# Accumulating transfers of a column pair's blocks, each tied to the low weight part of a later row pair

## The chip, the cores and the metric

The kernel runs on one core of a Trainium2 chip, written in Bass with the Tile layer. The metric is the device time of one execution in microseconds; the median of the runs counts. The kernel works in float32, which it splits into a high and a low part for TensorE.

## The reference

A two-layer decoder trunk on 256 tokens of width 2048: layer 0 is RetNet retention, layer 1 multi-head latent attention (MLA), each followed by a squared-ReLU MLP of width 8192, each added to the residual stream.

```python
for layer in range(DEPTH):                       # DEPTH = 2
    h = rms_norm(x, norm_mix[layer])
    if layer < N_A_LAYERS:
        x = x + retention(h, ret_w_in[layer], ret_w_out[layer], ret_cos, ret_sin)
    else:
        ...                                      # shared keys and values, once
        x = x + mla_attention(h, ...)
    x = x + sq_relu_mlp(rms_norm(x, norm_mlp[layer]), mlp_w1[layer], mlp_w2[layer])

def sq_relu_mlp(h, w1, w2):
    return jnp.square(jax.nn.relu(h @ w1)) @ w2
```

## The kernel before

All weights are streamed once from HBM, 479 MB in total, and every weight is split on the way: `split` makes a high part on ScalarE (line 184) and the low part, weight minus high part, on VectorE (line 185). TensorE then runs three matmuls for each product: high by high, high by low, low by high (lines 360 to 362).

Most products go through `gemm_pair`. It works on a *column pair*: 1024 output columns, two column blocks of 512, times two token blocks of 128, so four output blocks c11, c12, c21, c22. It goes through the inner dimension in *row pairs* of 256 rows, one call of `quad` each: one load of 1 MB (line 289, on the SyncE queue, three buffers `raw`), the split in parts, and the matmuls. A plain row pair has eight products, so 24 matmuls; a "seven" uses Strassen's scheme in the Winograd form, with seven products, 21 matmuls, and three sums of weight blocks on VectorE ahead of them (lines 319 to 324). Which row pairs are sevens stands in lists: `ODD` means the second, fourth, sixth and eighth, `SEVEN` the fourth, sixth and eighth, and so on.

At the end of a column pair `pair_out` copies the accumulators out of PSUM (line 377) and makes the sums of Winograd's form (lines 379 to 384). The result is two tiles for each of four blocks, eight tiles of 128 by 512, whose sums are the blocks. They lie in the pool `f2k`, 14 tiles that are used in turn.

The residual stream lives in HBM, in eight tiles `x_home` of 128 by 512. A product whose result isn't the last addition of its layer part is added there by `to_home`: eight transfers of 256 KB with an addition on the way (line 146), issued on GpSimd's queue, one for each tile. The result tiles of a column pair are sent by `send` in the order c11, c21, c12, c22, then the second tile of each. This is done for the first half of the retention's output product (name `ro0`, 2 column pairs) and for three of the four groups of each MLP's second product (names `d0_0` to `d1_2`, 2 column pairs each): 14 times eight transfers. For the last half or group the blocks of the residual stream are read back (`x_tiles`, line 138, also on GpSimd's queue) and added on VectorE (line 469).

What is issued when is set by a small clock. `later(n, fn)` puts a function into a list that is due n ticks on, and each row pair ends with one `tick`, which runs what is due. So the program hands out the eight transfers one per row pair, over the eight row pairs of the column pair that follows (`ro01`'s run under the next head's value and gate product, those of a group's second column pair under the next group's first up-projection `u`). The tick orders the program; what each engine's queue looks like in the end is also up to the Tile layer's scheduler. On the chip an instruction starts when it is first in its engine's queue and the semaphores it waits for have come.

GpSimd's queue holds little else: the norms' `rstd` (lines 162 and 164), the tables at the start, the reads and writes of `x_home`.

Of the kernel before, what the change touches and what calls it, by code (L numbers as in the profile page):

```python
# [16 lines left out]
ALU = mybir.AluOpType  # L17
# [49 lines left out]
def yoco(ctx: ExitStack, tc: tile.TileContext, a):  # L67
    nc = tc.nc
# [22 lines left out]
        return pool.tile([P, 2, 2, S], dtype, tag="act", bufs=24, name=name)  # L91


    queue = []
    clock, count = [0], itertools.count()

    def later(n, fn):
        queue.append((clock[0] + n, next(count), fn))
# [6 lines left out]
    def tick():  # L105
        clock[0] += 1
        while queue and min(q[0] for q in queue) <= clock[0]:
            run_first()
# [19 lines left out]
    x_home = [[dram.tile([P, 512], F32, name=f"xh_{t}_{b}") for b in range(NB)] for t in range(NT)]  # L128
# [14 lines left out]
    def to_home(c, p):  # L143

        def send(t, j, i):
            nc.gpsimd.dma_start(x_home[t][2 * p + j], c[t][j][i], accum_op=ALU.add)  # L146

        for n, (i, j, t) in enumerate(itertools.product(range(2), range(2), range(NT))):
            later(n, lambda i=i, j=j, t=t: send(t, j, i))
# [31 lines left out]
    def split(h, l, src, scale=None):  # L181

        if scale is None:
            nc.scalar.copy(h, src)  # L184
            return nc.vector.tensor_tensor(l, src, h.bitcast(F32), op=ALU.subtract)  # L185
        nc.scalar.activation(h, src, AF.Copy, scale=scale)
        return nc.vector.scalar_tensor_tensor(
            l, src, scale, h.bitcast(F32), op0=ALU.mult, op1=ALU.subtract
        )
# [16 lines left out]
    def stream(w, chunk, cols, name, use, done=None, before=None):  # L206

        raw = pool.tile([P, 2048], F32, tag="raw", bufs=3, name=f"{name}_raw")
        if before is None:
            nc.sync.dma_start(raw[:, :cols], w[chunk])  # L210
        n = cols // 2
        for half in range(2):
            wh = pool.tile([P, 1024], F32R, tag="wh", bufs=5, name=f"{name}_wh{half}")
            wl = pool.tile([P, 1024], F32R, tag="wl", bufs=5, name=f"{name}_wl{half}")
            cuts = 1
            if before is not None:
                cuts = 1 if half else 2
                m = n // cuts
                for i in range(cuts):
                    lo = half * n + i * m  # L220
                    nc.sync.dma_start(raw[:, lo : lo + m], w[chunk][:, lo : lo + m])
                    if i == 0:
                        before(half)
            m = n // cuts
            for i in range(cuts):
                lo = half * n + i * m
                split(wh[:, i * m : (i + 1) * m], wl[:, i * m : (i + 1) * m], raw[:, lo : lo + m])
            use(half, wh, wl)
        if done is not None:
            queue.append((clock[0] + 1, -1, done))  # L230
        tick()

    def piece(w, chunk, acc, act, g, nk, nb, name, before=None, done=None):

        if before is None:
            need(act, 2 * g + 2)

        def use(half, wh, wl):
            for j in range(2):
                k = g * 4 + half * 2 + j  # L240
                rh, rl = (v[:, j * nb : (j + 1) * nb] for v in (wh, wl))
                for t in range(NT):
                    ah, al = (act[k // 2][:, j, i, t * P : (t + 1) * P] for i in range(2))
                    nc.tensor.matmul(acc[t], ah, rh, start=k == 0, stop=False)
                    nc.tensor.matmul(acc[t], ah, rl, start=False, stop=False)
                    nc.tensor.matmul(acc[t], al, rh, start=False, stop=k == nk - 1)

        stream(
            w, chunk, 4 * nb, f"{name}{g}", use, done and (lambda: done(acc)),
            before and (lambda half: before(2 * g + half)),  # L250
        )

    def gemm_t(w, chunk0, act, nk, name, done):

        acc = accs(512, name)
        n = nk // 8
        for g in range(n):
            need(act, 4 * g + 4)

            def use(half, wh, wl):  # L260
                for j in range(4):
                    k = g * 8 + half * 4 + j
                    a = act[k // 2][:, k % 2]
                    for f in range(2):
                        cols = slice(j * 256 + f * P, j * 256 + (f + 1) * P)

                        def low():
                            nc.tensor.matmul(acc[f][:, 0:S], wl[:, cols], a[:, 0], start=False, stop=False)

                        if k > 0:  # L270
                            low()
                        nc.tensor.matmul(  # L272
                            acc[f], wh[:, cols], a.rearrange("p i s -> p (i s)"), start=k == 0, stop=k == nk - 1
                        )
                        if k == 0:
                            low()

            stream(w, chunk0 + g, 2048, f"{name}{g}", use, (lambda: done(acc)) if g == n - 1 else None)

    def queued_behind(ins, before):  # L280
        tc.add_manual_dep(
            ins.ins, before.ins.name,
            mybir.DependencyInfo(mybir.DependencyClass.NoSync, mybir.DependencyReason.DATA), reason="order",
        )

    def quad(w, chunk, x, mm, name):

        raw = pool.tile([P, 2048], F32, tag="raw", bufs=3, name=f"{name}_raw")
        nc.sync.dma_start(raw, w[chunk])
        v, more = x  # L290

        def a(t, k):
            return [v[:, k, i, t * P : (t + 1) * P] for i in range(2)]

        def s(n):
            return [more[:, n // 2, i, n % 2 * P : (n % 2 + 1) * P] for i in range(2)]

        def parts(src, n, part, after=None):
            wh = pool.tile([P, 1024], F32R, tag="wh", bufs=5, name=f"{name}_wh{part}")
            wl = pool.tile([P, 1024], F32R, tag="wl", bufs=5, name=f"{name}_wl{part}")  # L300
            low = split(wh[:, : n * 512], wl[:, : n * 512], src)
            if after is not None:
                queued_behind(low, after)
            return [[i[:, j * 512 : (j + 1) * 512] for i in (wh, wl)] for j in range(n)]

        if more is None:
            b11, b22 = parts(raw[:, 0:1024], 2, 0)
            mm("c11", a(0, 0), b11)
            mm("c21", a(1, 0), b11)
            mm("c12", a(0, 1), b22)  # L310
            mm("c22", a(1, 1), b22)
            b12, b21 = parts(raw[:, 1024:], 2, 1)
            mm("c12", a(0, 0), b12)
            mm("c22", a(1, 0), b12)
            mm("c11", a(0, 1), b21)
            mm("c21", a(1, 1), b21)
            return
        u = [pool.tile([P, 2, 512], F32, tag="us", bufs=2, name=f"{name}_u{i}") for i in range(2)]
        nc.vector.tensor_tensor(
            u[0], raw[:, 0:1024].rearrange("p (i n) -> p i n", i=2),  # L320
            raw[:, 1024:1536].unsqueeze(1).to_broadcast([P, 2, 512]), op=ALU.add,
        )
        nc.vector.tensor_tensor(u[1][:, 0], u[0][:, 0], raw[:, 512:1024], op=ALU.add)
        summed_up = nc.vector.tensor_tensor(u[1][:, 1], u[1][:, 0], raw[:, 1536:], op=ALU.add)  # L324
        b11, b22 = parts(raw[:, 0:1024], 2, 0, summed_up)
        mm("p1", a(0, 0), b11)
        mm("c12", s(3), b22)
        (b21,) = parts(raw[:, 1536:], 1, 1, summed_up)
        mm("c11", a(0, 1), b21)
        u2, u4 = parts(u[1].rearrange("p i n -> p (i n)"), 2, 2)  # L330
        mm("c21", a(1, 1), u4)
        mm("p6", s(2), u2)
        u1, u3 = parts(u[0].rearrange("p i n -> p (i n)"), 2, 3)
        mm("p5", s(1), u1)
        mm("p7", s(0), u3)
# [856 lines left out]
```

## Time and profile before

| | |
|---|---|
| runs (us) | 2511.81, 2500.82, 2499.96; median 2500.82 |
| profiled execution | 2506.1 us, span 2504.3 us |
| mean granted TensorE clock | 0.994 of full speed |
| busy share of TensorE, VectorE, ScalarE, GpSimd | 98%, 88%, 66%, 10% |
| read from HBM, written | 479.14 MB, 39.85 MB |
| accumulating transfers (line 146) | 112 of 256 KB |

How to read the rows: PE is TensorE, DVE VectorE, ACT ScalarE, POOL GpSimd, SP SyncE; a "q" behind the name is its queue of transfers. Times are in microseconds from the span's start. A timeline row gives start, length, engine, line, operation, output and inputs; in square brackets it has how long the engine stood idle before it and what ended that. A row of waits gives who waited for whom, then the total, the number of times and the longest. Buffer numbers and column pair numbers are left out of names, so `d_c` stands for every column pair of the second product, `u_c` for the first. A matmul's length is longer than its step, since matmuls overlap; the distance of two starts is what counts.

### The profile page before, as it was taken

To read this page: it belongs to the slowest core of one execution; us is meant where nothing else is said; L and a number is where in the kernel's file an instruction comes from. 1 tells how busy PE (TensorE), PEld (TensorE's weight loads), DVE (VectorE), ACT (ScalarE), POOL (GpSimd) and SP (SyncE) were. 2 spreads that over 40 slices of the span, in tenths; PEclk is the share of its full clock that TensorE was granted. 3 is DMA by queue.
4 is the path that set the end of the run, shared out by engine and by line. 5 is a ranking of instruction groups with operands and counts; after the bars stand their busy time and mean duration, and the time that the engine had idled before them with its cause. 6 is when DMAs were issued, how large, how long until landed. Compare 5 with 4: busy or idle time off the path is not lost.

```text
span 2504.3 us, 31661 instructions
## 1 busy us (share of the span) xinstructions
PE 2463.4 (98%) x11614; PEld 2069.5 (83%) x11614; DVE 2199.7 (88%) x2892; ACT 1648.3 (66%) x2297; POOL 251.6 (10%) x308
## 2 busy tenths in 40 slices
PE   9999999999999999999999999999999999999999
PEld 7788888888888878888788888998888788788787
DVE  6799999889889989989889998776999889899896
ACT  6566666556667757677667777666677567576673
POOL 7300011000010110110110101110000101101100
PEclk9999999999999999999999999999999999999999
DMA  8555577555565775775875555444556857857764
GB/s 310 191 200 189 189 220 243 193 188 208 202 233 183 217 251 183 235 231 194 239 249 200 195 194 180 161 147 160 190 200 206 243 203 213 251 184 226 241 214 167
DMA packets 93403, 521.04 MB, mean 208 GB/s; under 512 B 11072, under 2 KB 12224, under 8 KB 40000
## 3 DMA queue, kind: packets, MB, share of 16 engines
q1 hardware_dynamic: 71856, 472.83, 53.6%
q0 software_dynamic: 21248, 46.15, 9.5%
q8 instruction: 91, 1.49, 0.2%
q14 instruction: 64, 0.52, 0.1%
q10 hardware_dynamic: 144, 0.05, 0.0%
HBM read 479.14 MB, written 39.85 MB: 207 GB/s over the span
## 4 chain that ended last, share of the span: by engine, by line
PE 79%; DVE 10%; DMA 6%; ACT 2%; issue 2%; POOL 1%; DVEq 0%; ACTq 0%; POOLq 0%
PE u_c L361 6%; PE u_c L362 6%; PE u_c L360 6%; PE d_c L361 5%; PE d_c L362 5%; PE d_c L360 5%; DMA u_raw<-in_mlp_w 4%; PE rp_c L360 2%; PE rp_c L362 2%; PE rp_c L361 2%; PE rq_acc L272 2%; PE rk_acc L272 2%; DMA d_raw<-in_mlp_w 2%; DVE d_wl L185 2%; PE ro_c L361 1%
## 5 line engine op out<-in xcount | busy, mean ns | idle before, releaser
L185 DVE TENSOR_TENSOR d_wl<-d_raw,d_wh 128x1024 fp32r<-128x1024 f32 (+1 forms) x256 | 278.7, 1114 | 27.6 <-ACT d_wh L184 27.5
L184 ACT CAST d_wh<-d_raw 128x1024 fp32r<-128x1024 f32 (+1 forms) x256 | 241.6, 975 | 86.8 <-PE d_c L362 45.1
L185 DVE TENSOR_TENSOR u_wl<-u_raw,u_wh 128x1024 fp32r<-128x1024 f32 (+1 forms) x256 | 277.3, 1110 | 16.0 <-ACT u_wh L184 16.0
L361 PE MATMUL u_c<-u_wl,n 128*128 128x512 f32 x712 | 279.2, 392 | 11.1 <-DVE u_wl L185 11.1
L184 ACT CAST u_wh<-u_raw 128x1024 fp32r<-128x1024 f32 (+1 forms) x256 | 240.8, 971 | 74.5 <-PE u_c L362 48.9
L360 PE MATMUL u_c<-u_wh,n 128*128 128x512 f32 x712 | 279.8, 394 | 0.0
L362 PE MATMUL u_c<-u_wh,n 128*128 128x512 f32 x712 | 278.7, 391 | 0.0
L361 PE MATMUL d_c<-d_wl,hid 128*128 128x512 f32 x660 | 258.8, 392 | 6.5 <-DVE d_wl L185 6.5
L360 PE MATMUL d_c<-d_wh,hid 128*128 128x512 f32 x660 | 259.6, 393 | 0.0
L362 PE MATMUL d_c<-d_wh,hid 128*128 128x512 f32 x660 | 258.1, 391 | 0.0
L184 ACT CAST u_wh<-u_u 128x1024 fp32r<-128x1024 f32 x104 | 107.7, 1054 | 114.5 <-DVE u_u L324 60.4
L184 ACT CAST d_wh<-d_u 128x1024 fp32r<-128x1024 f32 x100 | 103.6, 1055 | 101.2 <-DVE d_u L324 54.1
L361 PEld LDWEIGHTS u_c<-u_wl,n 128*128 128x128 f32 x712 | 134.6, 189 | 42.0 <-DVE u_wl L185 14.7
L362 PEld LDWEIGHTS u_c<-u_wh,n 128*128 128x128 f32 x712 | 134.3, 189 | 27.9
L360 PEld LDWEIGHTS u_c<-u_wh,n 128*128 128x128 f32 x712 | 134.5, 189 | 27.5
L361 PEld LDWEIGHTS d_c<-d_wl,hid 128*128 128x128 f32 x660 | 124.7, 189 | 33.5 <-DVE d_wl L185 8.4
L184 ACT CAST rp_wh<-rp_raw 128x1024 fp32r<-128x1024 f32 x112 | 104.1, 946 | 68.8 <-PE rp_c L362 42.4
L362 PEld LDWEIGHTS d_c<-d_wh,hid 128*128 128x128 f32 x660 | 124.7, 189 | 26.0
L360 PEld LDWEIGHTS d_c<-d_wh,hid 128*128 128x128 f32 x660 | 124.7, 189 | 25.6
L185 DVE TENSOR_TENSOR u_wl<-u_u,u_wh 128x1024 fp32r<-128x1024 f32 x104 | 123.8, 1218 | 9.6 <-ACT u_wh L184 9.6
L146 POOL DMA_DIRECT2D xh<-d_c x48 | 41.9, 948 | 844.1 <-ACT d_c L377 843.7
L185 DVE TENSOR_TENSOR d_wl<-d_u,d_wh 128x1024 fp32r<-128x1024 f32 x100 | 119.0, 1218 | 5.0 <-ACT d_wh L184 5.0
(567 smaller groups left out, 6694.9 us busy)
## 6 DMA issues: line engine op xcount, KB each, us to landing
u_raw<-in_mlp_w SPq DMA_DIRECT2D x128, 1024.0 KB, 5.2
d_raw<-in_mlp_w SPq DMA_DIRECT2D x120, 1024.0 KB, 4.9
rp_raw<-in_ret_w_gv SPq DMA_DIRECT2D x56, 1024.0 KB, 4.9
ro_raw<-in_ret_w_out SPq DMA_DIRECT2D x32, 1024.0 KB, 5.0
uq_raw<-in_mla_w_uq SPq DMA_DIRECT2D x24, 768.0 KB, 4.2
rq_raw<-in_ret_w_qk SPq DMA_DIRECT2D x16, 1024.0 KB, 5.3
rk_raw<-in_ret_w_qk SPq DMA_DIRECT2D x16, 1024.0 KB, 4.8
xh<-d_c POOLq DMA_DIRECT2D x48, 256.0 KB, 5.5
```

Of the source, the lines that this page charges most:

```text
L146: nc.gpsimd.dma_start(x_home[t][2 * p + j], c[t][j][i], accum_op=ALU.add)
L184: nc.scalar.copy(h, src)
L185: return nc.vector.tensor_tensor(l, src, h.bitcast(F32), op=ALU.subtract)
L272: nc.tensor.matmul(acc[f], wh[:, cols], a.rearrange("p i s -> p (i s)"), start=k == 0, stop=k == nk - 1)
L360: nc.tensor.matmul(dst, ah, bh, start=n == 0, stop=False)
L361: nc.tensor.matmul(dst, ah, bl, start=False, stop=False)
L362: nc.tensor.matmul(dst, al, bh, start=False, stop=n == total[key] - 1)
```

## The change

`low_part` remembers the latest low part that `split` made of a weight in `quad` (and in `stream`, which the other products use). Each accumulating transfer gets a semaphore wait on that instruction. As `send` runs in the tick at the end of a row pair, each of the eight transfers waits for the last low part of its own row pair.

```diff
-    queue = []
+    queue, low_part = [], [None]
...
         def send(t, j, i):
-            nc.gpsimd.dma_start(x_home[t][2 * p + j], c[t][j][i], accum_op=ALU.add)
+            ins = nc.gpsimd.dma_start(x_home[t][2 * p + j], c[t][j][i], accum_op=ALU.add)
+            tc.add_manual_dep(
+                ins.ins, low_part[0].ins.name,
+                mybir.DependencyInfo(mybir.DependencyClass.Sync, mybir.DependencyReason.SCHED_ONLY), reason="spaced",
+            )
 
         for n, (i, j, t) in enumerate(itertools.product(range(2), range(2), range(NT))):
             later(n, lambda i=i, j=j, t=t: send(t, j, i))
...
-                split(wh[:, i * m : (i + 1) * m], wl[:, i * m : (i + 1) * m], raw[:, lo : lo + m])
+                low_part[0] = split(wh[:, i * m : (i + 1) * m], wl[:, i * m : (i + 1) * m], raw[:, lo : lo + m])
...
-            low = split(wh[:, : n * 512], wl[:, : n * 512], src)
+            low = low_part[0] = split(wh[:, : n * 512], wl[:, : n * 512], src)
```

The order in which instructions stand on TensorE, VectorE, ScalarE and SyncE is the same before and after. On GpSimd the transfers of a column pair stand in the order c11, c21, c12, c22; before, the scheduler had them as c22, c12, c11, c21.

## The prediction

> **What bounds the kernel now.** I read the page's first part, then who waited for whom on TensorE and VectorE, then the chain that ended last, then timelines and windows around the transfers.
>
> ```profile
> span 2504.3 us, 31661 instructions
> PE 2463.4 (98%) x11614; PEld 2069.5 (83%) x11614; DVE 2199.7 (88%) x2892; ACT 1648.3 (66%) x2297; POOL 251.6 (10%) x308
> PE u_c L361 <- DVE u_wl L185: 11.1, 8, 2.2
> PE d_c L361 <- DVE d_wl L185: 6.5, 4, 2.5
> DVE u_u L319 <- DMA u_raw<-in_mlp_w: 30.0, 18, 3.7
> DVE d_u L319 <- DMA d_raw<-in_mlp_w: 22.4, 15, 4.5
> ```
>
> TensorE sets the time: it is busy 98% of the span, so only what lets it run without a break can be won. In the two squared-ReLU MLPs it stands still 12 times, 17.6 us together, always for a low weight part of VectorE; and VectorE stands still there for a weight load (52.4 us in 33 waits). The next rows place one such stop: TensorE's timeline, VectorE's, the Pool queue's, and weight loads from the chain (start, length) with their usual landing time from the page's last part.
>
> ```profile
> 919.40 0.39 PE L362 MATMUL u_p<-u_wh,n_more 128*128 128x512 f32 x1
> 919.63 0.39 PE L360 MATMUL u_c<-u_wh,n 128*128 128x512 f32 x1
> 921.90 0.51 PE L361 MATMUL u_c<-u_wl,n 128*128 128x512 f32 x1 [1.88 <-DVE u_wl L185]
> 925.88 0.39 PE L362 MATMUL u_c<-u_wh,n 128*128 128x512 f32 x1
> ...
> 904.55 2.35 DVE L185 TENSOR_TENSOR u_wl<-u_u,u_wh 128x1024 fp32r<-128x1024 f32 x2
> ...
> 909.09 1.22 DVE L185 TENSOR_TENSOR u_wl<-u_raw,u_wh 128x1024 fp32r<-128x1024 f32 x1
> 918.76 1.23 DVE L319 TENSOR_TENSOR u_u<-u_raw 128x1024 f32<-128x1024 f32 x1 [3.12 <-DMA u_raw<-in_mlp_w]
> 920.63 2.35 DVE L185 TENSOR_TENSOR u_wl<-u_raw,u_wh 128x1024 fp32r<-128x1024 f32 x2
> ...
> 894.19 0.86 POOL L146 DMA_DIRECT2D xh<-d_c  x1 [23.17 <-ACT d_c L377]
> ...
> 905.99 1.56 POOL L146 DMA_DIRECT2D xh<-d_p  x1
> ...
> 910.34 8.33 DMA u_raw<-in_mlp_w
> 1209.78 9.59 DMA d_raw<-in_mlp_w
> 2348.37 7.72 DMA u_raw<-in_mlp_w
> ...
> u_raw<-in_mlp_w SPq DMA_DIRECT2D x128, 1024.0 KB, 5.2
> d_raw<-in_mlp_w SPq DMA_DIRECT2D x120, 1024.0 KB, 4.9
> ```
>
> The eight transfers of a column pair are issued within 12 us (894.19 to 905.99), though the program spaces them by row pairs: their data is ready, and nothing on Pool holds them back. The weight load that starts at 910.34, released by the low part that ends at 910.3, lands after 8.33 us where 4.9 to 5.2 is usual. VectorE reaches that row pair's sums early, waits 3.12 us, and makes the low part of the row pair in front only behind them (920.63); TensorE needs that one at 919.86 and stops.
>
> **The change part by part.** *What can be removed.* First the idle time, 17.6 us. Second, the restart: 919.63 to 921.90 is 2.27 us start to start against 0.23 for the step before it, so a stop costs 0.16 us more than its idle entry; 12 make 2.0. Third, the clock:
>
> ```profile
> core 0: us, PE busy (x) PEld busy (x) DVE busy (x) ACT busy (x) POOL busy (x), PEclk, DMA share, GB/s
> 900.00:905.00 5.00, 5.00 (x24) 4.14 (x23) 4.96 (x8) 3.10 (x5) 1.06 (x3) 1.00 1.07 245
> 920.00:925.00 5.00, 3.12 (x9) 2.48 (x9) 4.98 (x6) 1.39 (x2) 0.00 (x0) 0.73 0.23 48
> 1265.00:1270.00 5.00, 3.29 (x15) 2.50 (x14) 4.96 (x7) 1.61 (x3) 0.00 (x0) 1.00 0.95 314
> 1222.61 0.79 PE L361 MATMUL d_c<-d_wl,hid 128*128 128x512 f32 x1 [2.37 <-DVE d_wl L185]
> 1267.01 0.50 PE L361 MATMUL u_c<-u_wl,n 128*128 128x512 f32 x1 [1.71 <-DVE u_wl L185]
> 2359.33 0.50 PE L361 MATMUL u_c<-u_wl,n 128*128 128x512 f32 x1 [1.57 <-DVE u_wl L185]
> ```
>
> Behind the stop of 1.88 us the granted clock is 0.73; ten steps from 921.90 to 925.88 take 3.98 us instead of 2.27, 1.7 us lost. Behind the stop of 1.71 us it stays 1.00. Four stops of the twelve are of 1.88 us or more: 6.8 us. Together 17.6 + 2.0 + 6.8 = 26.4 us. The Trainium skill (TensorE: Matmul & The Clock Gate, Part 1) lets the clock halve only after an idle window of about 3.4 us; by it none of these stops could cost clock and the sum would be 19.6. The rows show otherwise, and the sum goes by them.
>
> *What the spacing does to a load.* No trace shows a single accumulating transfer beside weight loads, so its price is bounded. The queues in the stretch 894 to 922 us (packets, MB, share of 16 engines):
>
> ```profile
> q0 software_dynamic: 1152, 2.10, 48.0%
> q1 hardware_dynamic: 690, 4.99, 46.2%
> ```
>
> Eight transfers took 48.0% of 28 us, 13.4 us, or 1.7 us of all engines each; the loads took 12.9 us for 4.99 MB, 2.7 us per load of 1.05 MB. A row pair lasts 21 or 24 steps of 0.227 us, 4.8 or 5.4, 5.1 on average. In the burst the loads and transfers fill the engines (48.0 + 46.2 = 94%). With one transfer per row pair they need 2.7 + 1.7 = 4.4 of 5.1 us, 86%, so nothing piles up. A load that meets one transfer lands 0 to 1.7 us later: 4.9 to 6.9 us. The change makes a low part release a transfer and a load together (the low part that ends at 910.3 would release both), so I take the upper half, 6.0 to 6.9.
>
> *What a load may take.* 8.33 us cost an idle 1.88, so 6.45 us would have cost none; in the same way 9.59 − 2.37 = 7.2, and 7.72 − 1.57 = 6.15. So a tight load has 6.2 to 7.2 us. Against 6.0 to 6.9 most loads are in time and the worst are up to 0.7 us late. That is under the 1.71 us at which the clock held. I take an average of 0.4 us, restart included, for each of some 12 loads as tight as these: 5 us stay.
>
> *The wait itself.* Pool has the same 112 transfers to issue. Each now waits for VectorE's count of the last low part of the row pair in whose turn it is issued; the built order also becomes c11, c21, c12, c22 instead of c22, c12, c11, c21. No instruction moves on the other four engines. Queued behind the waits on Pool are reads of the residual and a few norm factors:
>
> ```profile
> 1254.85 3.21 POOL L138 DMA_DIRECT2D x_mlp<-xh  x4
> L480 POOL DMA_DIRECT2D xh<-x_mlp x8: 539/539/544, 1376.2 to 1425.6; - x8
> 430.07 2.35 DVE L185 TENSOR_TENSOR rp_wl<-rp_u,rp_wh 128x1024 fp32r<-128x1024 f32 x2
> 448.88 0.60 ACT L179 ACTIVATE o_sq<-o 128x512 bf16<-128x512 f32 x1
> 937.66 1.23 DVE L185 TENSOR_TENSOR u_wl<-u_u,u_wh 128x1024 fp32r<-128x1024 f32 x1 [1.39 <-ACT u_wh L184]
> 957.41 0.42 DVE L400 TENSOR_TENSOR hid_sum<-hid_u 128x256 f32<-128x256 f32 x1
> xh<-d_p POOLq DMA_DIRECT2D x24, 256.0 KB, 9.9
> ```
>
> The transfers ahead of the reads then last eight row pairs of 5.1 us, not 12 us, so the reads start some 30 us later than 1254.85; their blocks are written home from 1376.2 on, so 90 us cover that. In the retention part the last transfer waits for the low part ending at 432.4, and the next norm factor's input comes at 448.9. Block tiles are held longer. The tightest reuse: a last transfer is released at 938.9, and with the burst's 9.9 us to landing it is done at 949.7; its tile is next written at 957.41. The margin is 7.7 us, without it a stop of VectorE. All this costs nothing, so the sum is −26.4 + 5 = −21 us.
>
> The profiled execution took 2506.1 us, 1.8 outside its span; it becomes 2485. That execution is 5.3 above the median of the runs, 2500.8, which becomes **2480 us**, −0.8%.
>
> **The rivals.** *The delay only spreads out.* Under 13.4 us of transfers the loads are delayed by 13.4 us of engine time in either order, and 14 windows of four summed row pairs give 56 tight loads instead of 12. If a load needs the full 6.9 us and half of them have the shorter 6.2, 28 stops of 0.7 us make 20 us, and only the clock and some idle time are won: −7 us, 2494. For it speaks that the shares are as good as equal, 48.0 and 46.2%: a long software queue does not take more than its half. The Trainium skill has that as a rule (DMA: Bandwidth & Descriptors, Queues, rings and completion order): each engine goes round the queues that have work, packet by packet, and the rows agree. By it a burst slows loads only while it lasts, and spacing makes more loads share. Against this rival is the 14% of engine time left over.
>
> *A tight load meets two transfers.* Two last low parts can end 3.4 us apart (904.55 + 2.35 = 906.9, then 910.3), and the transfer before is still in flight. Then a load takes 4.9 + 3.4 = 8.3 us, the burst's own figure, 1.7 us above what it has, and stops TensorE for 1.9 with the restart. It decides from 14 of the 56 loads on, where 14 × 1.9 = 27 eats up the gain; at 26 of them the kernel is 23 us slower, 2523. Against it: it needs the next load within a transfer's landing in nearly half of the cases.
>
> *The wait is already over.* For the first two transfers of a window the low part is older than the data. If that held for all, nothing would change: 2501. The last one waits until 938.9 where the burst's last is issued at 905.99, so this is unlikely.
>
> **How the numbers follow.** The forecast, stops mostly gone, 2472 to 2488: 0.64. Spread delay, 2488 to 2503: 0.19. Two transfers: 0.11. Wait over: 0.06. About 0.5% is what a measurement of this kernel can tell from no change, 12.5 us: faster means under 2488. Faster 0.64, same 0.19 + 0.06 = 0.25, slower 0.11. The range starts where all 26.4 us and a spare 6 go, 2468 (the runs differ by that much and more), and ends at 2503, which takes in the spread delay and the empty wait. The forecast's own range is 2472 to 2488.
>
> **What would show it.** The Pool rows of a window 894 to 940 stand some 5 us apart from the third on. Weight loads in the chain are 7 us or shorter. TensorE's two waits for low parts fall from 17.6 us to 5 or less, none above 1.7 us, and no window outside the start has a clock under 0.9 that now has one from a stop. VectorE's waits for weight loads get smaller and no more. The prediction is wrong if loads of 8 us stay, or if VectorE or ScalarE waits for a transfer's landing.

## The result

The changed kernel takes 2484.42 us (median of 5 runs, 2477.23 to 2490.05), the kernel before 2500.82 (5 runs, 2499.96 to 2511.81). The ratio is 0.9921, with a 95% interval of 0.9891 to 0.9950: 16.4 us less. The profiled execution took 2490.05 us with a span of 2488.3 us, 16.0 less than the span before. Line numbers behind 146 have moved by four: `split`'s low part is now line 189, the three matmuls of `gemm_pair` lines 364 to 366, the sums of weight blocks 323 to 328. The experiments shift them by up to four lines more; the kernel without transfers has those of before.

These are the rows that answer to those of before: from the page its head, the first part and two rows of transfers with their usual landing times; then who waited for whom (total, times, longest).

```profile
span 2488.3 us, 31679 instructions
PE 2457.3 (99%) x11614; PEld 2066.6 (83%) x11614; DVE 2198.9 (88%) x2892; ACT 1648.2 (66%) x2297; POOL 251.4 (10%) x308
...
u_raw<-in_mlp_w SPq DMA_DIRECT2D x128, 1024.0 KB, 5.5
d_raw<-in_mlp_w SPq DMA_DIRECT2D x120, 1024.0 KB, 5.0
```

```profile
PE d_c L365 <- DVE d_wl L189: 3.0, 3, 1.3
PE u_c L365 <- DVE u_wl L189: 2.8, 3, 1.4
PE ro_c L365 <- DVE ro_wl L189: 1.6, 2, 1.3
PE rp_c L365 <- DVE rp_wl L189: 0.8, 1, 0.8
...
DVE u_u L323 <- DMA u_raw<-in_mlp_w: 23.1, 19, 3.1
DVE d_u L323 <- DMA d_raw<-in_mlp_w: 19.1, 12, 3.3
...
POOL xh L146 <- DVE u_wl L189: 184.8, 43, 6.5
POOL xh L146 <- DVE d_wl L189: 177.1, 41, 6.7
```

The work of every engine is the same to 1%; only TensorE's standing still has shrunk. In the MLPs it waits 5.8 us in 6 stops for a low part, where it was 17.6 us in 12. VectorE's waits for weight loads have shrunk much less, from 52.4 to 42.2 us, and the usual landing time of a load has not fallen at all. The 84 waits of Pool for a low part say that the added semaphores do hold the transfers back. No engine waits for a transfer's landing that it did not wait for before.

Pool's timeline in the window that the prediction named, long loads of the chain (start, length; first the two longest, of the retention part, then the longest five of the MLPs), and the four places where the granted clock fell before:

```profile
904.96 0.86 POOL L146 DMA_DIRECT2D xh<-d_c  x1 [6.20 <-DVE u_wl L189]
911.27 0.86 POOL L146 DMA_DIRECT2D xh<-d_c  x1 [5.44 <-DVE u_wl L189]
914.67 0.86 POOL L146 DMA_DIRECT2D xh<-d_c  x1 [2.54 <-DVE u_wl L189]
920.01 0.86 POOL L146 DMA_DIRECT2D xh<-d_c  x1 [4.47 <-DVE u_wl L189]
...
939.65 0.86 POOL L146 DMA_DIRECT2D xh<-d_p  x1 [3.75 <-DVE u_wl L189]
```

```profile
358.43 9.82 DMA ro_raw<-in_ret_w_out
402.05 8.70 DMA rp_raw<-in_ret_w_gv
...
1041.12 8.52 DMA d_raw<-in_mlp_w
1094.88 7.59 DMA u_raw<-in_mlp_w
1942.37 7.86 DMA d_raw<-in_mlp_w
1985.00 7.26 DMA u_raw<-in_mlp_w
2280.92 8.25 DMA d_raw<-in_mlp_w
```

```profile
core 0: us, PE busy (x) PEld busy (x) DVE busy (x) ACT busy (x) POOL busy (x), PEclk, DMA share, GB/s
920.00:925.00 5.00, 4.55 (x21) 3.44 (x20) 4.21 (x5) 2.49 (x3) 0.86 (x1) 1.00 0.94 290
1220.00:1225.00 5.00, 5.00 (x24) 4.14 (x23) 5.00 (x7) 3.27 (x4) 0.86 (x1) 1.00 0.77 202
1955.00:1960.00 5.00, 5.00 (x24) 4.12 (x23) 4.16 (x5) 3.03 (x3) 1.24 (x2) 1.00 0.86 245
2170.00:2175.00 5.00, 5.00 (x24) 4.14 (x23) 4.97 (x6) 3.37 (x5) 0.86 (x2) 1.00 0.86 262
```

The clock holds at these places now, and in all stages with transfers; it still falls at 89.5 us and in the attention part, where none run. Counted from start to start of the matmuls, with restarts and clock, the stops around the transfers cost 27.4 us before and 10.6 after: 16.8 of difference, against 16.0 in the span. So the gain is the stops, and what is left of them is twice what was forecast. MLP loads of 7 to 8.5 us are still there, and in the retention part one of 9.82 us. The experiments ask why.

### The profile page after: what moved, and what is told of

The parts are those of the page before. It is cut to its first block, busy times and chain, and to the rows that moved or that the text cites. A ratio compares the mean times of both kernels' runs of the same rounds, so it can differ in the third digit from the quotient of the medians.

```text
span 2488.3 us, 31679 instructions
## 1 busy us (share of the span) xinstructions
PE 2457.3 (99%) x11614; PEld 2066.6 (83%) x11614; DVE 2198.9 (88%) x2892; ACT 1648.2 (66%) x2297; POOL 251.4 (10%) x308
## 4 chain that ended last, share of the span: by engine, by line
PE 86%; DVE 7%; DMA 3%; ACT 2%; issue 1%; POOL 1%; DVEq 0%; ACTq 0%; POOLq 0%
PE u_c L365 6%; PE u_c L366 6%; PE u_c L364 6%; PE d_c L365 6%; PE d_c L366 6%; PE d_c L364 6%; PE rq_acc L276 2%; PE rp_c L364 2%; PE rp_c L365 2%; PE rp_c L366 2%; PE rk_acc L276 2%; PE u_p L364 2%; PE u_p L365 2%; PE u_p L366 2%; PE d_p L364 2%; PE d_p L366 2%
## 5 line engine op out<-in xcount | busy, mean ns | idle before, releaser
L189 DVE TENSOR_TENSOR rp_wl<-rp_raw,rp_wh 128x1024 fp32r<-128x1024 f32 x112 | 118.8, 1089 | 5.3 <-ACT rp_wh L188 5.0
```

## The experiments

Twelve runs, on three chips. A *tight load* below is the one that a plain row pair's last low part releases: its data go to a seven, whose sums VectorE reaches early. The load that follows it some 2 to 4 us later has more time. The *lead* of a transfer is how long before a tight load's issue it is issued. "Stops" are TensorE's waits for low parts in the stages with transfers, from the table of waits; one of 0.7 to 0.8 us in the retention part (`rp_p`) is in the kernel without transfers too and isn't counted. The table sums up; the text takes the runs in turn. Each ratio is against the kernel before on the same chip.

| kernel | median us | ratio, 95% interval | stops us | VectorE's waits for MLP loads us |
|---|---|---|---|---|
| before | 2500.8 | 1 | 17.9 | 52.4 |
| changed kernel | 2484.4 | 0.9921 (0.9891–0.9950) | 8.2 | 42.2 |
| changed kernel again | 2481.9 | 0.9919 (0.9895–0.9943) | 7.7 | 37.3 |
| no transfers | 2473.6 | 0.9883 (0.9853–0.9913) | 0.0 | 3.1 |
| one wait for all eight | 2501.4 | 0.9991 (0.9977–1.0005) | 18.7 | 53.0 |
| pairs, seven's last low part | 2482.4 | 0.9911 (0.9890–0.9933) | 4.8 | 38.5 |
| pairs, plain's last | 2478.8 | 0.9895 (0.9870–0.9921) | 1.3 | 16.5 |
| the same again | 2475.6 | 0.9891 (0.9865–0.9916) | 0.4 | 14.8 |
| pairs, plain's first | 2514.1 | 1.0046 (1.0032–1.0061) | 30.1 | 74.1 |
| pairs, seven's first | 2475.6 | 0.9891 (0.9868–0.9913) | 1.4 | 19.2 |
| singles, plain's last and seven's first | 2477.8 | 0.9893 (0.9868–0.9919) | 2.1 | 10.1 |
| singles, plain's first and seven's last | 2485.0 | 0.9923 (0.9901–0.9946) | 4.4 | 38.9 |
| pairs, plain's first, no accumulation | 2478.5 | 0.9899 (0.9870–0.9927) | 1.9 | 20.0 |
| fours, plain's last | 2481.1 | 0.9912 (0.9889–0.9935) | 2.9 | 38.1 |

Two profiled executions of one and the same kernel differ by 3.3 us (spans 2477.7 and 2474.4, pairs at the plain's last low part), so smaller differences between single rows are not read.

**No transfers at all.** In `send`:

```diff
-            nc.gpsimd.dma_start(x_home[t][2 * p + j], c[t][j][i], accum_op=ALU.add)
+            pass
```

> The kernel before without the 112 accumulating transfers of the column pairs (the sums never reach the residual stream in HBM; all else is computed). Theory: the stops of TensorE in those windows come from weight loads that share the 16 DMA engines with the transfers; then all of them go, about -27 us against before, waits of TensorE for low parts in the windows under 1 us, no load above 6.5 us in the chain there. Rival (order or wait): the 16 us of the change come from the order of the queue or from the wait, not from shared engines; then taking the traffic away brings something else than the whole loss, less than 20 us.

2473.61 us, 29.3 less than the kernel before on that chip. Its rows of waits for loads:

```profile
DVE d_u L319 <- DMA d_raw<-in_mlp_w: 1.6, 1, 1.6
DVE u_u L319 <- DMA u_raw<-in_mlp_w: 1.5, 4, 0.5
```

52.4 us of VectorE's waits are 3.1 without the transfers, and TensorE waits for no low part in these stages. So the transfers cause all these stops, and some 29 us is the most that an arrangement of them can bring. Not all of it need be theirs. In the profiled executions the spans differ by 32.6 us, and nearly 4 of them arise in the attention part, between the two MLPs, where no accumulating transfer runs: the clock there is granted at half for 13.7 us before and for 3.4 us here. What is left, 28.7 us, is near the prediction's sum of 26.4 us, made from stops alone.

**One wait for all eight.** The transfers wait for the low part of the first row pair only, so they have the changed kernel's semaphores and order, but are no longer spaced by row pairs:

```diff
+        first = low_part[0]
+
...
-                ins.ins, low_part[0].ins.name,
+                ins.ins, first.ins.name,
```

> As changed, but all eight transfers of a column pair wait for the low part of the first row pair: same order of the queue, same kind of wait, no spacing. Theory: a burst again, loads of 8 to 10 us, 12 or so stops, within 4 us of before. Rival (order or wait): keeps the gain, -16 us.

2501.44 us, no change. TensorE's stops are back:

```profile
PE u_c L367 <- DVE u_wl L191: 11.2, 7, 2.2
PE d_c L367 <- DVE d_wl L191: 5.7, 6, 1.3
```

The eight go out within 14 us of one another (905.60 to 919.14 in one window). So neither the order c11, c21, c12, c22 nor a wait as such does it. The gain is from the spacing.

**Pairs: at the sevens or at the plain rows.** `low_part` is set by every second row pair alone, so two transfers go out together after each of them:

```diff
-            low = low_part[0] = split(wh[:, : n * 512], wl[:, : n * 512], src)
+            low = split(wh[:, : n * 512], wl[:, : n * 512], src)
+            if more is not None:        # sevens; "more is None" for plain rows
+                low_part[0] = low
```

> As changed, but only sevens set the low part that a transfer waits for: the transfers go in pairs, behind every second row pair, away from the moment when a plain row pair's last low part releases the tight load. Theory (the phase counts: after the change a tight load still meets two transfers, 1041.12 to 1049.6): the tight load now meets at most the tail of a pair, stops under 4 us in all, -20 to -26 us against before. Rival (only the rate counts): two at a time is nearer to the burst, so less gain than the change, -6 to -14 us.

> As changed, but only plain row pairs set the low part that a transfer waits for: the same rate as behind the sevens, two transfers at each tight load's release. Theory (the phase counts): each tight load meets two transfers, 8 us and more, so most of the gain goes, -6 to +6 us against before, more than the other pairing by 15 us or more. Rival (only the rate counts): the same time as behind the sevens within 4 us.

I had the two instants the wrong way round. The pairs at the sevens come out level with the changed kernel (2482.35 us); those at the plain rows, which are released together with a tight load, look better (2478.79 us), which the run on one chip below bears out. Pool's, SyncE's and VectorE's rows of the plain kernel place one:

```profile
1036.43 1.75 POOL L146 DMA_DIRECT2D xh<-d_c  x2 [8.41 <-DVE d_wl L189]
1036.16 0.33 SPq L293 DMA_DIRECT2D d_raw<-in_mlp_w  x1
1041.98 1.23 DVE L325 TENSOR_TENSOR d_u<-d_raw 128x1024 f32<-128x1024 f32 x1 [0.51 <-DMA d_raw<-in_mlp_w]
```

Two transfers are issued 0.3 us behind the tight load, and it is in after 5.8 us, where a tight load has 6.2 to 7.2. In the other kernel the sevens' pairs of the same stretch are issued 3.1 to 5.2 us ahead of a tight load, and its chain holds loads of 8.18 and 7.63 us elsewhere. So a new theory: what is issued ahead of a tight load, by a little, goes in front of it.

**The instant alone.** The same pairs, with the first instead of the last low part of the same row pair:

```diff
-            if more is None:
+            if more is None and part == 0:          # and the same for sevens
                 low_part[0] = low
```

> As the kernel in which a plain row pair's last low part sets the wait, but its first low part sets it: the pairs of transfers are issued about 2 us before the tight load's issue, not 0.3 us after it. Theory of phase: a transfer delays the tight load when its data move while the load's do, so one issued 2 to 3 us ahead of the load costs, and one issued with it comes behind the load's data and costs little. Then loads of 7.5 to 9 us at these places, 6 to 15 us of TensorE waits for low parts, 2482 to 2488 us. Theory of pairs: it only counts that every second tight load meets a transfer at all, whatever the instant. Then as the kernel with the plain rows' last low parts: one stop or two, 2478 to 2481 us.

> As the kernel in which the sevens' last low part sets the wait, but a seven's first low part sets it: the pairs of transfers are issued about 3 us sooner, some 7 to 8 us before the next tight load and at the issue of the second load. Theory of phase: by the tight load they have landed (6 us), so few stops: under 3 us of them, 2477 to 2480 us. Theory of pairs: as with the sevens' last low part, 6 to 7 us of stops and 2481 to 2484 us.

2514.07 us and 2475.56 us. Moving the pairs of the plain rows 1 to 2 us forward makes a kernel that was 1.1% faster 0.5% slower than before: in the MLPs the first of a pair is now issued 0.9 to 2.0 us ahead of the tight load at most places, and no longer 0.3 us behind it. The same place in that kernel, and its waits:

```profile
1041.51 1.75 POOL L146 DMA_DIRECT2D xh<-d_c  x2 [7.46 <-DVE d_wl L189]
1043.51 0.33 SPq L293 DMA_DIRECT2D d_raw<-in_mlp_w  x1
1051.01 1.23 DVE L325 TENSOR_TENSOR d_u<-d_raw 128x1024 f32<-128x1024 f32 x1 [2.20 <-DMA d_raw<-in_mlp_w]
...
PE u_c L367 <- DVE u_wl L189: 21.6, 15, 4.0
PE d_c L367 <- DVE d_wl L189: 6.6, 9, 1.7
```

The lead is 2.0 us here, the load takes 7.5, and there are 24 stops in the MLPs. The sevens' pairs, moved forward to a lead of some 6 to 8 us, have the opposite effect:

```profile
PE u_c L367 <- DVE u_wl L189: 0.9, 2, 0.7
PE d_c L367 <- DVE d_wl L189: 0.5, 1, 0.5
```

Who lands first can be read in the part on transfers of the window 890 to 930 us (usual landing time last). First the pairs at the plain's last low part, then those at its first:

```profile
u_raw<-in_mlp_w SPq DMA_DIRECT2D x8, 1024.0 KB, 6.3
xh<-d_c POOLq DMA_DIRECT2D x4, 256.0 KB, 7.5
```

```profile
u_raw<-in_mlp_w SPq DMA_DIRECT2D x8, 1024.0 KB, 7.4
xh<-d_c POOLq DMA_DIRECT2D x4, 256.0 KB, 5.5
```

It is an exchange: the transfers of `d_c` land 2 us sooner, and the loads pay for it with 1.1 us each. Behind a load, a transfer's later landing costs nothing, since nobody waits for it. The Trainium skill (DMA: Bandwidth & Descriptors, Queues, rings and completion order) says that each engine goes round the queues that have work, packet by packet. The exchange fits that, and the rule's other half shows in it: the turns are shared only among queues that have work at that moment, so a transfer 2 us ahead has the engines to itself for that time. That is argued from the landing times; no run shows the turns themselves.

**Both again, on one chip.** 

> The kernel in which only plain row pairs' last low parts set the wait, beside the changed kernel on one chip. Theory of phase and theory of pairs alike: 2477 to 2481 us, 3 to 8 us less than the changed kernel.

> The changed kernel beside the four-in-pairs kernels on one chip: 2482 to 2487 us by every theory; it is there so that differences of 3 to 8 us are read on one chip.

2475.56 us (5 runs, 2474.87 to 2477.12) against 2481.88 (6 runs, 2478.47 to 2491.35): the pairs at the plain rows' last low parts are 6.3 us faster than the changed kernel, and no run of one lies among the other's. This kernel and the one with pairs at the sevens' first low part lie 2 us from the kernel without transfers.

**Singles, good and bad instants.** One transfer per row pair as in the changed kernel. The good one moves only the sevens' instant, from the last low part to the first; the bad one only the plain rows':

```diff
+            if part == (1 if more is None else 0):      # bad: (0 if more is None else 3)
+                low_part[0] = low
```

> One transfer per row pair as in the changed kernel, but a seven's first low part sets the wait and not its last; a plain pair's last low part as before. So only the instant of every second transfer moves, about 3 us sooner, from some 3 to 4 us ahead of a tight load to some 6 to 7 us ahead. Theory of phase: the stops go, under 3 us of TensorE waits for low parts in the window stages, 2474 to 2478 us. Theory of pairs (transfers in twos leave every second tight load free): as the changed kernel, some 10 us of stops, 2481 to 2486 us.

> One transfer per row pair, a plain pair's first low part and a seven's last set the wait, so each transfer is issued 2 to 4 us ahead of a tight load. Theory of phase: every tight load of these stages takes 7 us or more, 15 to 35 us of stops, 2490 to 2512 us. Theory of pairs: as the changed kernel, 2481 to 2486 us.

The good kernel takes 2477.78 us, and all its MLP stops are gone; what is left is in the retention stage:

```profile
PE ro_c L367 <- DVE ro_wl L189: 2.1, 2, 2.0
```

So in the changed kernel the MLP stops come from the transfers at the sevens' last low part. The bad kernel takes 2485.01 us, less than the 2490 to 2512 that I expected; the stops are 4.4 us, not 15 to 35. One transfer ahead of a tight load isn't two: as an estimate, its 1.7 us and the usual 4.9 make 6.6, inside the 6.2 to 7.2 that the load has. That doesn't settle each load. At some places the seven's transfer is still in flight as well, 3.1 us ahead beside the plain row's 2.0; there the load of 1039.78 took 7.38 us, and that of 1082.56, with the same two leads, 5.88. So the instant counts and the number of transfers too, but what else makes one load late and not another is not shown.

Of its 2485 only some 5 us lie in stops. Most of the rest can be placed in the profiled executions: against the pairs at the sevens' first low part (spans 2484.7 and 2475.4 us), 4.6 us arise in the attention part, where no such transfer runs and the clock is granted at half for 13.7 us here and for 3.4 us there. A few microseconds between two rows of the table can thus have nothing to do with the transfers.

**The same bad instant without accumulation.** As the pairs at the plain's first low part, with plain writes:

```diff
-            ins = nc.gpsimd.dma_start(x_home[t][2 * p + j], c[t][j][i], accum_op=ALU.add)
+            ins = nc.gpsimd.dma_start(x_home[t][2 * p + j], c[t][j][i])
```

> The kernel in which a plain pair's first low part sets the wait (2514 us), with its transfers written without accumulation (the blocks replace what is in memory and are not added). If the delay is the accumulating transfers' own length: loads of 6 us or less, under 8 us of stops, 2476 to 2484 us. If any transfer of 256 KB at that instant delays the load alike: 2505 to 2516 us.

2478.53 us: 36 us less than with accumulation, at the same instant and for the same bytes to write. The queues in the same stretch 1041 to 1051 us, first with accumulation, then without (packets, MB, share of 16 engines):

```profile
q0 software_dynamic: 288, 0.52, 34.6%
```

```profile
q0 software_dynamic: 148, 0.52, 14.1%
```

Of 10 us these are 3.5 and 1.4 us for two transfers. The accumulation more than doubles what a transfer takes from the loads, with twice the packets.

**Fours.** Only every second plain row pair sets `low_part`:

```diff
+            if more is None and part:
+                plains[0] += 1
+                if plains[0] % 2:
+                    low_part[0] = low
```

> Only every second plain row pair's last low part sets the wait: the transfers go out in fours, 0.3 us after a tight load's issue, so seldom but in half as many places as with pairs. Four transfers need about 7 us of the 16 DMA engines and the next tight load is 10 us later. Theory of phase alone: as with pairs, 2475 to 2480 us. If the size of the burst counts as well: the load behind them is late, 5 to 15 us of stops, 2482 to 2495 us.

2481.13 us, between the two forecasts: stops of 2.9 us, and VectorE's waits for MLP loads are 38.1 us where the pairs have 15 to 17. Four transfers behind a tight load, some 7 us of the engines at 1.7 us each, seem to reach into the next loads still; no row here follows one of them.

## Why the prediction was right, and where not

The direction and the cause hold. *The loss that can be removed*, 26.4 us worked out from idle time, restart and clock, is borne out by the kernel without transfers, 29 us and 28.7 in the spans without the attention part. *The clock* is a part of it as costed: in the stages with transfers no stop of 1.88 us or more is left in the changed kernel's first profile and the granted clock holds at all four places (its second run has one such stop, shown at the end). *The wait itself* cost nothing, as forecast: Pool's rows stand 4.6 to 5.3 us apart from the third on, and no engine waits for a held tile, a late read of the residual or a norm factor.

The step that was mis-sized is *what the spacing does to a load*, with the 5 us that stay. They are 10.6 us in the profiled execution, and the gain is 16 us instead of 21: not twelve loads late by 0.4 us on average but nine stops of 1.2 us. The text let a tight load meet one transfer and land after 6.0 to 6.9 us. In the changed kernel one can meet two. The load of 1041.12 took 8.52 us; transfers were issued at 1037.98, by a seven's last low part, and 1041.39, by the plain row's that releases the load itself, 3.4 us apart. By the experiments it is the one ahead that costs: with the sevens' instant alone moved, the MLP stops are gone. Yet the load of 1085.00 stands between two transfers with the same two leads and took 5.54 us, so the instant makes a load's delay likely and doesn't fix it. The average share, 86% of the engines, was right (57.9% for the loads and 28.5% for the transfers from 890 to 930 us) but does not say when within a row pair the transfer comes. Of what would show the forecast wrong, the loads of 8 us did stay; low part waits of 5.8 us instead of 5 and a longest of 1.4 are just about what was forecast. In the retention stage the waits even grew, from 0.3 to 2.4 us, and its longest load of the chain from 7.96 to 9.82 us.

I also took it that a transfer released together with the load would hurt, and therefore took the upper half of the range of delays. The pairs at the plain's last low part show that this is the harmless instant, and the one 1 to 2 us sooner the harmful one.

*Two transfers at a tight load*, the rival of 0.11, has its mechanism seen, with 8.52 us against its 8.3, and its condition missed: the changed kernel's MLPs have 6 stops and not 14. The kernel with pairs just ahead has 24 there, loads of up to 9.7 us in the chain, and is 11 us slower than before, where the rival's working gives 27 us to be eaten up at 14 loads and 2523 us at 26. *The delay only spreads out* fails: VectorE's waits for loads shrank by a fifth in the changed kernel and by some two thirds in the best ones with pairs and the same number of transfers, so the delays do not merely move. The price of 1.7 us per transfer stands: 3.5 us for two in the window above. *The wait is already over* falls with Pool's 84 waits, and an effect of the new order with the kernel of one wait, which changes nothing.

Not settled is the retention stage. The good singles stop there still, behind a load of 8.10 us whose nearest transfers are issued 0.3 and 2.0 us after it, and the pairs at the plain rows, with 0.3 and 0.8, have no such stop. Nor was a kernel with a fourth load buffer run, which would take the tightness away instead of the transfers.

## What to carry to other kernels

When background transfers share the DMA engines with loads that have little slack, it isn't enough that the engines have time left over on average: tie the transfer to the event that also releases the tight load, or to one that lies a whole landing time ahead of it, and not to one a little ahead, least of all two transfers at once. Try both sides of such an instant before settling for a spacing; here, for pairs, 1 to 2 us decided between 1.1% faster and 0.5% slower. Count an accumulating transfer at more than twice a plain write of the same size, as here (3.5 us of the engines against 1.4 for two).

## What the hardware showed unexpectedly

A stop of the same length may or may not cost clock. The kernel with pairs at the plain's first low part has a stop of 2.21 us that ends at 925.84, the changed kernel's second run one of 2.22 us that ends at 415.27. Behind the first the clock stays at 1.00, behind the second it falls to half. The clock's records of these traces show why: every change of the clock within a trace lies on one grid with steps of 3.41 us. These are the windows of that grid around the two stops (for the first, counted back from a fall at 2009.76). Their columns are those of the windows above: length, busy time of the five engines with TensorE first, clock, share of the DMA engines and GB/s:

```profile
924.32:927.73 3.41, 1.89 (x8) 1.60 (x9) 3.41 (x5) 0.10 (x1) 1.65 (x2) 1.00 0.10 12
927.73:931.15 3.42, 3.42 (x16) 2.83 (x16) 3.42 (x4) 2.01 (x2) 0.10 (x1) 1.00 1.03 271
```

```profile
411.64:415.06 3.42, 1.40 (x7) 0.82 (x5) 2.90 (x3) 1.57 (x2) 0.00 (x0) 1.00 0.87 166
415.06:418.47 3.41, 3.20 (x8) 2.53 (x9) 3.41 (x5) 1.04 (x1) 0.86 (x1) 0.50 0.49 67
```

The first stop is cut by a border of the grid: at most 1.52 us of idleness fall into one window, and the next keeps the full clock. Of the second, 2.01 us fall into one window, and the next has half the clock. In the kernel before, the stop of 1.88 us lay whole in one window and cost clock; the stop of 1.71 us lay whole in one and did not. So the prediction's border between 1.71 and 1.88 us is one for the idleness within a window and not for the length of a stop: from 1.88 to 2.2 us it can go either way. It isn't sharp, since elsewhere in these traces 1.70 to 1.75 us in one window go either way. The Trainium skill (TensorE: Matmul & The Clock Gate, Part 1) calls the window in which idleness is judged free-running and about 3.4 us long; the grid of these traces agrees with both. That a whole window must be idle is not borne out, since about half of one was enough.
